# Routing a transformer block's experts by token halves, with the router's product in four column groups

## The chip, the cores and the metric

One NeuronCore of a Trainium2 chip runs the whole program. The metric is the device time of one execution, in microseconds, as the median of several runs.

## The reference

One encoder block over 256 tokens of width 1024, in fp32. The first part (projections, three attention branches, gates) ends in an output projection and a residual sum; the second part is a mixture of 16 experts in four groups, of which each token uses two of one group:

```
x = x + (g_ret * y_ret + g_na * y_na + g_xa * y_xa) @ w_out
t = rmsnorm(x, g_ffn)
grp = top_1(softmax(t @ w_rg + b_rg))                 # 4 groups
in_grp = (t @ w_re + b_re)[grp's 4 experts]
top_w, top_idx = top_2(softmax(in_grp)), weights rescaled to sum 1, times the group's weight
out = sum over the chosen experts e of  weight_e * (silu(t @ w_gate[e]) * (t @ w_up[e])) @ w_down[e]
x = rmsnorm(x + out, g_final)
```

w_gate and w_up are 16 x 1024 x 512, w_down is 16 x 512 x 1024: 100.7 MB of weights in fp32, read once.

## The kernel before

Products of the first part are made in three fp32r matmuls of a high and a low part. ScalarE rounds a tile to its high part, VectorE subtracts to get the low one; the raw weights go through some ten buffers, the converted ones through five ("h").

The stretch of the change begins with the output projection. `wout(q, pts)` (line 868) multiplies a quarter q of the contraction for both token halves (a = 0, 1; 128 tokens each) into PSUM, 12 matmuls of 512 columns. It runs four quarters for the first 512 output columns (n = 0) and four for the second (n = 1). For each half of the columns and of the tokens, `x1_sum` (881) adds the residual on VectorE, `x1_sq` (885) squares on ScalarE for the norm, `x1_T` (889) transposes four 128 x 128 blocks on TensorE, `x1_ev` (894) copies them out on ScalarE, and `logits` (897) multiplies them with the router weights: 128 columns of tokens are the stationary operand, 32 columns of router weights (20 used) the moving one. `x1_rstd` (949) makes 1/rms on VectorE and GpSimd. `seed` (904) multiplies x1 by the identity into the four PSUM accumulators that the experts' results are added to.

Then comes the routing. `route(a)` (1011) is a chain of twelve small VectorE operations for one token half: scale the logits, take the best group, select its experts, take the best two, make a 0/1 mask. The two halves are interleaved (1041). Matmuls with a triangle of ones count positions (1048), and `select(g)` (1105) turns them into a 0/1 matrix of tokens by slots, 64 slots for each of a group's four experts. `gather` (1116) multiplies the normed x1 (a high and a low part, `normed_hi` and `normed_lo`, 977 and 981) with it: 16 matmuls for the high part, 16 for the low one, and ScalarE and VectorE scale the result by the gain into `xg`.

The expert loop `experts` (1286) takes two experts at a time. `gate_up` (1183) makes gate and up products side by side: gate in the array's columns 0 to 63, up in 64 to 127, in plain fp32. Then ScalarE's Silu and VectorE's product write `gs` (1198, 1199), `hidden` (1235) transposes it, `down` (1202) multiplies by w_down, `weigh` (1225) weighs and splits, `scatter` (1244) adds to the accumulators. At the end `finish` (1257) norms and writes out.

Inside this stretch every engine runs its instructions in the order written (`manual_schedule`). Expert weights come by SP's queue in a fixed order of units of 1 MB, each into one of about 20 buffers: `fetch(tag)` (139) issues the next unit into the buffer just released, so an issue waits for the last matmul that reads the buffer. A unit of gate and up weights is 256 rows of both, two transfers of 512 KB with 2 KB runs (`rows_in`, 147; `gate_and_up`, 767). A unit of w_down is 256 rows, with 4 KB runs.

Of the kernel before, what the change touches and what calls it, by code (L numbers as in the profile page):

```python
# [30 lines left out]
def hybrid_encoder_kernel(  # L31
# [694 lines left out]
    V.memset(wr, 0.0)  # L726
    tc.keep_in_program_order(nc.sync.dma_start(wr[:, :, 16:20], w_rg[0].rearrange("(k p) n -> p k n", p=P)))
# [36 lines left out]
    def expert_units():  # L764
        us = []

        def gate_and_up(e, r):
            def go(raw):
                for h, w in ((0, w_gate), (1024, w_up)):
                    rows_in(w[e, r : r + 256])(raw[:, h : h + 1024])  # L770

            return go
# [95 lines left out]
    def wout(q, pts):  # L868
        w = halves.pop(0)
        for a in range(2):  # L870
            ts = slice(a * P, (a + 1) * P)
            for k in range(2):
                kk = 2 * q + k
                PE.matmul(pts[a], m_hi[kk // 4][:, kk % 4, ts], w[k][0], start=kk == 0, stop=False)
                PE.matmul(pts[a], m_hi[kk // 4][:, kk % 4, ts], w[k][1], start=False, stop=False)
                PE.matmul(pts[a], m_lo[kk // 4][:, kk % 4, ts], w[k][0], start=False, stop=kk == KT - 1)
        if not parts:
            hl_tags.remove(w[2])
            fetch(w[2])
# [30 lines left out]
    for q in range(4):  # L910
        if q < 2:
            mt = mixed_T(1, q)
        wout(q, p0)
        if q < 2:
            mixed(1, q, mt)
        feed()
# [6 lines left out]
    rlog = [bank([P, 32]) for _ in range(2)]  # L923
    p1 = [pj([P, 512]) for _ in range(2)]
    xt = [bank([P, 4, P]) for _ in range(2)]
    x1T[0] = tmp([P, 4, 256])
    x1_sum(0, 0, p0)
    x1_sum(0, 1, p0)
    x1_sq(0, 0)
    x1_sq(0, 1)  # L930
    wout(0, p1)
    feed()
    wout(1, p1)
    fetch("A0")
    x1_T(0, 0, xt[0])
    x1_T(0, 1, xt[1])
    feed()
    x1_ev(0, 0, xt[0])
    x1_ev(0, 1, xt[1])
    wout(2, p1)  # L940
    logits(0, 0)
    logits(0, 1)
    feed()
    wout(3, p1)
    xt = [pj([P, 4, P]) for _ in range(2)]
    x1T[1] = tmp([P, 4, 256])
# [7 lines left out]
    x1_sum(1, 0, p1)  # L954
    fetch("E0")
    x1_T(1, 0, xt[0])
    x1_sq(1, 0)
    x1_ev(1, 0, xt[0])
    x1_sum(1, 1, p1)
    x1_rstd(0)  # L960
    x1_T(1, 1, xt[1])
    logits(1, 0)
    x1_sq(1, 1)
    x1_ev(1, 1, xt[1])
    logits(1, 1)
    x1_rstd(1)
    tx.close()
    tpx.close()
    fp = ctx.enter_context(tc.tile_pool(name="fp", bufs=1))
    for tag in ("T0", "T1"):  # L970
        home[tag] = fp
        fetch(tag)
# [13 lines left out]

    for a in range(2):
        for n in range(2):
            normed_hi(a, n)
            seed(x1, a, n)  # L990
    show("x1", x1)
# [19 lines left out]
    def route(a):  # L1011
        V.scalar_tensor_tensor(lgt[:, a, 0:20], rlog[a][:, :20], r2[:, a : a + 1], rb, op0=ALU.mult, op1=ALU.add)
        yield
        V.max(gval[:, a], lgt[:, a, 16:24])
        yield
        V.max_index(gidx[:, a], gval[:, a], lgt[:, a, 16:24])
        yield
        V.tensor_tensor(ohg[:, a], io4, gidx[:, a, 0:1].to_broadcast([P, 4]), op=ALU.is_equal)
        yield
# [6 lines left out]
        yield  # L1026
        V.tensor_reduce(pad[:, a, 0:4], sel[:, a].rearrange("p g e -> p e g"), axis=AX.X, op=ALU.add)
        yield
        V.max(eval_[:, a], pad[:, a])
        yield  # L1030
        V.max_index(eidx[:, a], eval_[:, a], pad[:, a])
        yield
        for i in range(2):
            V.tensor_tensor(oh[:, i, a], io4, eidx[:, a, i : i + 1].to_broadcast([P, 4]), op=ALU.is_equal)
        yield
        V.tensor_add(m4[:, a], oh[:, 0, a], oh[:, 1, a])
        yield
        spread(msk, m4, a)
        yield

    rt = [route(a) for a in range(2)]
    for i in range(16):
        if i < 11:
            next(rt[0])
        if i >= 5:
            next(rt[1])
    pp = bank([P, 3, 16])
    for o, pieces in (
        (pp[:, 0], ((tri, 0),)),
        (pp[:, 1], ((tri, 1), (ones, 0))),  # L1050
        (pp[:, 2], ((ones, 0), (ones, 1))),
    ):
# [10 lines left out]
    e21 = tiny(2, tag="e21")  # L1063
    V.tensor_sub(e21, eval_[:, :, 1], eval_[:, :, 0])
    A.activation(e21, e21, AF.Exp)
    A.activation(warm, e21[:, 0:1], AF.Silu)
    V.tensor_add(posm, posm, pp[:, 0:2])
    cmax = tiny(1, tag="cmax")

    def counts():  # L1070
        V.tensor_reduce(cmax, pp[:, 2], axis=AX.X, op=ALU.max)

# [30 lines left out]
    counts()  # L1103

    def select(g):
        pd = slot("X", [P, 2, 4, SLOTS], F32R)
        for a in range(2):
            V.tensor_tensor(
                pd[:, a],
                posm[:, a, 4 * g : 4 * g + 4].unsqueeze(2).to_broadcast([P, 4, SLOTS]),  # L1110
                iota.unsqueeze(1).to_broadcast([P, 4, SLOTS]),
                op=ALU.is_equal,
            )
        return pd

    def gather(pd, lead=False):
        pts = [bank([P, 2, 256]) for _ in range(4)]

        def part(u, x, first):
            for j in range(2):  # L1120
                ks = slice((2 * u + j) * P, (2 * u + j + 1) * P)
                for a in range(2):
                    PE.matmul(
                        pts[u][:, j],
                        x[:, a, ks],
                        pd[:, a].rearrange("p e s -> p (e s)"),
                        start=first and j + a == 0,
# [298 lines left out]
```

## Time and profile before

| | |
|---|---|
| median of 3 runs | 545.36 us (545.16 to 545.42) |
| the profiled execution | 545.44 us, span 543.5 us |
| PE (TensorE matmuls) busy | 528.5 us, 97% of the span |
| DVE (VectorE) busy | 264.3 us, 49% |
| ACT (ScalarE) busy | 229.0 us, 42% |
| granted TensorE clock, mean | 0.994 of full speed |
| moved by DMA | 159.91 MB, mean 294 GB/s, over 400 GB/s in most slices of the expert loop |

PE's busy time comes from pipelined matmuls whose ends are modelled: the distance between the starts of two matmuls tells more than the duration of one. PEld is the loading of weights into the array. A row of the timeline gives the start in us, the duration, engine, line and operation, output and inputs by the program's names, sizes, how many instructions of the kind are merged (x4), and in brackets how long the engine stood idle before and who released it. Names are cut: "b" and "pj" are PSUM tiles, "C" is x1 or xg, "h", "A", "E", "G", "r" are buffers of weights. L12 is line 12 of the kernel.

### The profile page before, as it was taken

The page shows a single profiled execution, that of the slowest core. Times are in us where ns is not written, and L with a number is a line of the kernel's source. Part 1 is how long each engine was busy: PE and PEld are TensorE (multiplying, and loading weights), DVE is VectorE, ACT ScalarE, POOL GpSimd, SP SyncE. Part 2 cuts the span into 40 slices and gives each one's busy share as a digit, 9 for nine tenths or more (in the row PEclk, how much of TensorE's full clock was granted, in tenths as well). Part 3 has the DMA queues.
Part 4 walks back from the last instruction along what each step waited for, and adds up shares of the span by engine and source line. Part 5 has one row for each costly group of instructions (what it writes and reads, how often), then busy time and mean ns, then how long its engine had stood idle before and what let it go on. Part 6 is the DMA issues. An engine that isn't in the chain of part 4 may idle for free. (4 is left out here: it accounts for less than half of the span.)

```text
span 543.5 us, 7482 instructions
## 1 busy us (share of the span) xinstructions
PE 528.5 (97%) x2912; PEld 359.9 (66%) x2912; DVE 264.3 (49%) x461; ACT 229.0 (42%) x378; POOL 18.5 (3%) x21
## 2 busy tenths in 40 slices
PE   8999999999999999999999999999999999999992
PEld 6999899967778888888888863353435343534340
DVE  6598798995657768384566171130112111210122
ACT  6775566698654464544535261121111111111123
POOL 0005000040000000000000000000000000000000
PEclk9999999999999999999999999999999999999997
DMA  8987778045445799739983799999999999999962
GB/s 302 390 316 233 224 147 256 17 156 163 148 154 189 235 334 301 257 103 403 354 318 151 275 344 330 416 406 418 406 414 409 409 413 407 416 406 418 406 242 81
DMA packets 89815, 159.91 MB, mean 294 GB/s; under 512 B 13104, under 2 KB 27824, under 8 KB 89776
## 3 DMA queue, kind: packets, MB, share of 16 engines
q1 hardware_dynamic: 89056, 158.80, 80.1%
q10 hardware_dynamic: 720, 0.58, 0.3%
q8 instruction: 25, 0.41, 0.3%
q14 instruction: 14, 0.11, 0.1%
HBM read 158.32 MB, written 1.05 MB: 293 GB/s over the span
## 5 line engine op out<-in xcount | busy, mean ns | idle before, releaser
L129 DVE TENSOR_TENSOR h<-r,h 128x1024 fp32r<-128x1024 f32 x58 | 71.2, 1239 | 31.6 <-ACT h L128 31.2
L128 ACT CAST h<-r 128x1024 fp32r<-128x1024 f32 x58 | 60.2, 1048 | 23.4 <-PE pj L308 12.5
L306 PE MATMUL pj<-h,A 128*128 128x512 f32 x160 | 63.1, 394 | 0.0
L308 PE MATMUL pj<-h,A 128*128 128x512 f32 x160 | 62.7, 392 | 0.0
L307 PE MATMUL pj<-h,A 128*128 128x512 f32 x160 | 62.6, 391 | 0.0
L1199 DVE TENSOR_TENSOR gs<-gs,b 64x512 f32<-64x512 f32 x16 | 11.1, 691 | 87.1 <-ACT gs L1198 87.1
L288 PE MATMUL pj<-A,h 128*128 128x256 f32 x160 | 45.7, 286 | 0.0
L290 PE MATMUL pj<-A,h 128*128 128x256 f32 x160 | 45.5, 284 | 0.0
L289 PE MATMUL pj<-A,h 128*128 128x256 f32 x160 | 45.3, 283 | 0.0
L308 PEld LDWEIGHTS pj<-h,A 128*128 128x128 f32 x160 | 30.1, 188 | 6.9 <-issue 0.8
L306 PEld LDWEIGHTS pj<-h,A 128*128 128x128 f32 x160 | 30.1, 188 | 6.7 <-issue 0.4
L307 PEld LDWEIGHTS pj<-h,A 128*128 128x128 f32 x160 | 30.1, 188 | 6.3 <-DVE h L129 0.4
L1230 DVE SCALAR_TENSOR_TENSOR os<-b,c,os 128x512 fp32r<-128x512 f32 x16 | 12.0, 751 | 41.9 <-ACT os L1229 41.0
L1198 ACT ACTIVATE gs<-b 64x512 f32<-64x512 f32 x16 | 9.4, 588 | 51.8 <-PE b L1191 51.8
L288 PEld LDWEIGHTS pj<-A,h 128*128 128x128 f32 x160 | 30.7, 192 | 0.1
L290 PEld LDWEIGHTS pj<-A,h 128*128 128x128 f32 x160 | 30.7, 192 | 0.1
L289 PEld LDWEIGHTS pj<-A,h 128*128 128x128 f32 x160 | 30.7, 192 | 0.1
L129 DVE TENSOR_TENSOR h<-G,h 128x1024 fp32r<-128x1024 f32 x18 | 24.1, 1346 | 10.3 <-ACT h L128 9.8
L1229 ACT ACTIVATE os<-b,c 128x512 fp32r<-128x512 f32 x16 | 11.0, 687 | 40.6 <-PE b L1210 39.7
L1191 PE MATMUL b<-h,C 128*64 128x512 f32 x104 | 24.0, 592 | 0.0
L128 ACT CAST h<-G 128x1024 fp32r<-128x1024 f32 x18 | 18.8, 1049 | 10.6 <-PE pj L308 9.3
L1210 PE MATMUL b<-h,hh 128*64 128x512 f32 x64 | 21.3, 592 | 0.0
(327 smaller groups left out, 1029.3 us busy)
## 6 DMA issues: line engine op xcount, KB each, us to landing
r<-in_w_in_dram SPq DMA_DIRECT2D x20, 1024.0 KB, 5.4
h<-in_w_exp_down_dram SPq DMA_DIRECT2D x10, 1024.0 KB, 11.5
h<-in_w_exp_gate_dram SPq DMA_DIRECT2D x13, 512.0 KB, 11.0
h<-in_w_exp_up_dram SPq DMA_DIRECT2D x13, 512.0 KB, 11.1
r<-in_w_exp_down_dram SPq DMA_DIRECT2D x6, 1024.0 KB, 11.6
A<-in_w_exp_down_dram SPq DMA_DIRECT2D x5, 1024.0 KB, 11.4
r<-in_w_exp_gate_dram SPq DMA_DIRECT2D x9, 512.0 KB, 10.2
r<-in_w_exp_up_dram SPq DMA_DIRECT2D x9, 512.0 KB, 10.3
```

Of the source, the lines that this page charges most:

```text
L128: pin(A.copy(hi, part))
L129: pin(V.tensor_sub(lo, part, hi.bitcast(F32)))
L288: PE.matmul(pt, whi[:, cs], thi[:, k], start=k == 0, stop=False)
L289: PE.matmul(pt, whi[:, cs], tlo[:, k], start=False, stop=False)
L290: PE.matmul(pt, wlo[:, cs], thi[:, k], start=False, stop=k == kn - 1)
L306: PE.matmul(pts[a], thi[:, kk, ts], whi, start=first, stop=False)
L307: PE.matmul(pts[a], thi[:, kk, ts], wlo, start=False, stop=False)
L308: PE.matmul(pts[a], tlo[:, kk, ts], whi, start=False, stop=last)
L1191: PE.matmul(pt[c * 64 : c * 64 + 64], xg[:, k, p % 2 * 2 + i], w[:, 2 * c + j], start=k == 0, stop=k == KT - 1)
L1199: V.tensor_mul(gs[i * 64 : i * 64 + 64], gs[64:128], pt[64:128])
L1210: PE.matmul(pts[n][i * 64 : i * 64 + 64], hh[:, 2 * u + k], ws[i][1][:, k, ns], start=u + k == 0, stop=u + k == 2)
L1230: V.scalar_tensor_tensor(o[:, 1], pt, c, o[:, 0].bitcast(F32), op0=ALU.mult, op1=ALU.subtract)
```

## The change

- The second column half of the output projection goes by token halves: all four quarters for half 0 (with the first half's transposes and logits between them), then quarters 1 to 3 for half 1.
- The router's product swaps its operands: 32 columns of router weights are stationary, 128 tokens move, and the four blocks of a column half go to the four groups of 32 array columns. `bound` copies the four partial sums out (ScalarE) and adds them by one more matmul, which also turns them back.
- `route(0)` is put before `route(1)`, no longer interleaved, and three quarters of half 0's gather are put ahead of `route(1)`. The four PSUM banks of the gather ("lead") hold the logits, the positions and the transposes before. Seeds are cut into 256 columns and put at other places.
- Expert weights are read in 8 KB runs: a unit is 512 rows of gate or of up weights, partition p holding rows 4p to 4p+3, and w_down likewise. `gate_up` takes two units at a time and releases both behind eight matmuls. To match, the normed x1 and the gate/up results are written in permuted order, read at a stride of four elements (`fours`). The gain in that order, `gx`, is loaded in eight small transfers.

The diff, cut:

```
-    def rows_in(src, parts=1):
+    def runs_in(src, parts=1):
         def go(raw):
-            dst = raw.rearrange("p (k n) -> p k n", n=src.shape[1])
+            dst = raw.rearrange("p (k n) -> p k n", n=src.shape[2])
             k = dst.shape[1] // parts
-            for i in range(parts):
-                feeder[0].dma_start(
-                    dst[:, i * k : i * k + k], src[i * k * P : (i + 1) * k * P].rearrange("(k p) n -> p k n", p=P)
-                )
+            for i in range(0, dst.shape[1], k):
+                feeder[0].dma_start(dst[:, i : i + k], src[:, i : i + k])
 
         return go
...
     V.memset(wr, 0.0)
+    gx = cp.tile([P, KT], F32, name="gx")
+    for q in range(4):
+        src = gains.rearrange("(p j) c -> p j c", j=4)
+        for u in range(2):
+            pin(nc.sync.dma_start(gx[q * 32 : q * 32 + 32, 4 * u : 4 * u + 4], src[:, :, 24 + 4 * u + q]))
...
         def gu(e):
-            us.extend(gate_and_up(e, r) for r in range(0, D, 256))
+            for r in (0, 512):
+                us.extend(runs_in(w[e, r : r + 512].rearrange("(p j) n -> p j n", j=4)) for w in (w_gate, w_up))
+
+        def by_four(e):
+            return w_down[e].rearrange("(p k) n -> p k n", k=4)
 
         def dn(*es):
-            for r in (0, 256):
-                us.extend(rows_in(w_down[e, r : r + 256]) for e in es)
+            for k in (0, 2):
+                us.extend(runs_in(by_four(e)[:, k : k + 2]) for e in es)
 
         def dn_cols(e):
             for c in (0, 512):
-                us.append(rows_in(w_down[e, :, c : c + 512], 2 if c and e == NE - 1 else 1))
+                us.append(runs_in(by_four(e)[:, :, c : c + 512], 2 if c and e == NE - 1 else 1))
...
+    def wout(q, pts, w, a, ks=(0, 1)):
+        ts = slice(a * P, (a + 1) * P)
+        for k in ks:
+            kk = 2 * q + k
+            PE.matmul(pts[a], m_hi[kk // 4][:, kk % 4, ts], w[k][0], start=kk == 0, stop=False)
+            PE.matmul(pts[a], m_hi[kk // 4][:, kk % 4, ts], w[k][1], start=False, stop=False)
+            PE.matmul(pts[a], m_lo[kk // 4][:, kk % 4, ts], w[k][0], start=False, stop=kk == KT - 1)
+
+    def used(w):
+        hl_tags.remove(w[2])
+        fetch(w[2])
...
     def logits(n, a):
         for j in range(4):
             k = 4 * n + j
-            PE.matmul(rlog[a], x1T[n][:, j, a * P : (a + 1) * P], wr[:, k], start=k == 0, stop=k == KT - 1)
-
-    acc = [[None, None], [None, None]]
-
-    def seed(base, a, n):
-        acc[a][n] = acc[a][n] or pj([P, 512])
-        PE.matmul(acc[a][n], ident, base[:, a, n * 512 : n * 512 + 512], start=True, stop=False)
+            PE.matmul(
+                sheaf[a][32 * j : 32 * j + 32],
+                wr[:, k],
+                x1T[n][:, j, a * P : (a + 1) * P],
+                start=not n,
+                stop=bool(n),
+            )
+
+    def bound(a):
+        A.copy(sheaves[:, a], sheaf[a])
+        PE.matmul(rlog[a], sheaves[:, a], four, start=True, stop=True)
...
+    lead = [bank([P, 512]) for _ in range(4)]
+    spare = lead[3]
+    rlog = [lead[0][:, 32:64], spare[:, 32:64]]
+    pp = [lead[0][:, 0:16], spare[:, 64:80], spare[:, 80:96]]
+    sheaf = [b[:, 128:256] for b in (lead[0], spare)]
+    sheaves = cp.tile([P, 2, P], F32, name="sheaves")
+    four = cp.tile([P, 32], F32, name="four")
+    for g in range(4):
+        gs = slice(32 * g, 32 * g + 32)
+        A.copy(four[gs], ident[gs, gs])
+    xt = [b.rearrange("p (j t) -> p j t", j=4) for b in lead]
...
+    acc = [[p0[a], p1[a]] for a in range(2)]
+
+    def seed(base, a, n, hs=(0, 1)):
+        for h in hs:
+            cs = slice(h * 256, h * 256 + 256)
+            PE.matmul(acc[a][n][:, cs], ident, base[:, a, n * 512 + h * 256 : n * 512 + h * 256 + 256], start=not h, stop=False)
+
+    for n in range(2):
+        x1T[n] = tmp([P, 4, 256])
...
+    def fours(t):
+        return t.rearrange("q (p j) -> q j p", j=4)
+
+    def by_p(t):
+        return t.rearrange("q (j p) -> q j p", j=4)
+
     def normed_hi(a, n):
         ns = slice(n * 512, n * 512 + 512)
-        A.activation(x1_hi[:, a, ns], x1[:, a, ns], AF.Copy, scale=r2[:, a : a + 1])
+        A.activation(by_p(x1_hi[:, a, ns]), fours(x1[:, a, ns]), AF.Copy, scale=r2[:, a : a + 1])
 
     def normed_lo(a, n):
         ns = slice(n * 512, n * 512 + 512)
         V.scalar_tensor_tensor(
-            x1_lo[:, a, ns], x1[:, a, ns], r2[:, a : a + 1], x1_hi[:, a, ns].bitcast(F32), op0=ALU.mult, op1=ALU.subtract
+            by_p(x1_lo[:, a, ns]),
+            fours(x1[:, a, ns]),
+            r2[:, a : a + 1],
+            by_p(x1_hi[:, a, ns].bitcast(F32)),
+            op0=ALU.mult,
+            op1=ALU.subtract,
         )
...
+    def settled(a):
+        V.scalar_tensor_tensor(posm[:, a], msk[:, a], 1e6, pp[a], op0=ALU.mult, op1=ALU.add)
+
+    def chosen(pd, g, a):
+        V.tensor_tensor(
+            pd[:, a],
+            posm[:, a, 4 * g : 4 * g + 4].unsqueeze(2).to_broadcast([P, 4, SLOTS]),
+            iota.unsqueeze(1).to_broadcast([P, 4, SLOTS]),
+            op=ALU.is_equal,
+        )
+
+    def part(pt, u, x, pd, a, first, last):
+        pt = pt.rearrange("p (j c) -> p j c", j=2)
+        for j in range(2):
+            k = 2 * u + j
+            PE.matmul(
+                pt[:, j],
+                x[:, a, k * P : (k + 1) * P],
+                pd[:, a].rearrange("p e s -> p (e s)"),
+                start=first and not j,
+                stop=last and j == 1,
+            )
...
+    for a in range(2):
+        x1_sum(0, a, p0)
+        x1_sq(0, a)
+    ws = [halves.pop(0)]
+    for a in range(2):
+        wout(0, p1, ws[0], a)
+    used(ws[0])
+    feed()
+    ws += halves
+    wout(1, p1, ws[1], 0)
+    for a in range(2):
+        x1_T(0, a, xt[a])
+        x1_ev(0, a, xt[a])
+    wout(2, p1, ws[2], 0)
+    wout(3, p1, ws[3], 0)
+    for a in range(2):
+        logits(0, a)
+    x1_sum(1, 0, p1)
+    x1_sq(1, 0)
+    x1_rstd(0)
+    wout(1, p1, ws[1], 1)
+    used(ws[1])
+    fetch("A0")
+    x1_T(1, 0, xt[2])
+    x1_ev(1, 0, xt[2])
+    for n in range(2):
+        normed_hi(0, n)
+        normed_lo(0, n)
+    wout(2, p1, ws[2], 1)
+    used(ws[2])
+    logits(1, 0)
+    wout(3, p1, ws[3], 1, (0,))
+    bound(0)
+    wout(3, p1, ws[3], 1, (1,))
+    used(ws[3])
+    fetch("E0")
+    x1_sum(1, 1, p1)
+    x1_sq(1, 1)
+    route(0)
+    x1_rstd(1)
+    seed(x1, 0, 0)
+    x1_T(1, 1, xt[1])
+    x1_ev(1, 1, xt[1])
+    seed(x1, 1, 0)
+    logits(1, 1)
+    PE.matmul(pp[0], tri, msk[:, 0], start=True, stop=True)
+    pd0 = slot("X", [P, 2, 4, SLOTS], F32R)
+    settled(0)
+    chosen(pd0, 0, 0)
+    bound(1)
+    tx.close()
+    tpx.close()
+    fp = ctx.enter_context(tc.tile_pool(name="fp", bufs=1))
+    for tag in ("T0", "T1"):
+        home[tag] = fp
+        fetch(tag)
+    for u in range(3):
+        for x in (x1_hi, x1_lo):
+            part(lead[u], u, x, pd0, 0, x is x1_hi, False)
+    for n in range(2):
+        normed_hi(1, n)
+    route(1)
+    for o, pieces in ((pp[1], ((tri, 1), (ones, 0))), (pp[2], ((ones, 0), (ones, 1)))):
         for i, (l, a) in enumerate(pieces):
-            PE.matmul(o, l, msk[:, a], start=i == 0, stop=i == len(pieces) - 1)
-    posm = cp.tile([P, 2, 16], F32, name="posm")
-    V.tensor_scalar(posm, msk, 1e6, -1e6, op0=ALU.mult, op1=ALU.add)
+            PE.matmul(o, l, msk[:, a], start=i == 0, stop=i == 1)
+    settled(1)
+    counts()
+    chosen(pd0, 0, 1)
+    part(spare, 3, x1_hi, pd0, 0, True, False)
+    part(spare, 3, x1_lo, pd0, 0, False, False)
+    for u in range(4):
+        part(lead[u], u, x1_hi, pd0, 1, False, False)
+    for a in range(2):
+        seed(x1, a, 1)
     gneg = tiny(2, tag="gneg")
     V.tensor_scalar_mul(gneg, gval[:, :, 0], -1.0)
+    e21 = tiny(2, tag="e21")
+    V.tensor_sub(e21, eval_[:, :, 1], eval_[:, :, 0])
+    for n in range(2):
+        normed_lo(1, n)
+    for u in range(4):
+        part(lead[u], u, x1_lo, pd0, 1, False, True)
...
+            for x in () if done else (x1_hi, x1_lo):
+                for a in range(2):
+                    part(pt, u, x, pd, a, x is x1_hi and a == 0, x is x1_lo and a == 1)
+            pt = pt.rearrange("p (j c) -> p j c", j=2)
+            if bool(u % 2) != bool(done):
                 for j in range(2):
                     k = 2 * u + j
                     A.activation(
-                        xg[:, k].rearrange("p e s -> p (e s)"), pt[:, j], AF.Copy, scale=gt[:, 3, k : k + 1]
+                        xg[:, k].rearrange("p e s -> p (e s)"), pt[:, j], AF.Copy, scale=gx[:, k : k + 1]
...
     def gate_up(xg, i, p, gs, between=None):
         pt = bank([P, DFF])
         for u in range(2):
-            for h in range(2):
-                tag, w = take(DFF)
-                for j in range(2):
-                    k = 4 * u + 2 * h + j
-                    for c in range(2):
-                        PE.matmul(
-                            pt[c * 64 : c * 64 + 64], xg[:, k, p % 2 * 2 + i], w[:, 2 * c + j], start=k == 0, stop=k == KT - 1
-                        )
+            ws = [take(DFF) for _ in range(2)]
+            for k in range(4 * u, 4 * u + 4):
+                for c in range(2):
+                    PE.matmul(
+                        pt[c * 64 : c * 64 + 64], xg[:, k, p % 2 * 2 + i], ws[c][1][:, k % 4], start=k == 0, stop=k == KT - 1
+                    )
+            for tag, _ in ws:
                 fetch(tag)
             if between and not u:
                 between()
         gs = gs or keep([P, DFF], "gs")
-        A.activation(gs[64:128], pt[0:64], AF.Silu)
-        V.tensor_mul(gs[i * 64 : i * 64 + 64], gs[64:128], pt[64:128])
+        A.activation(by_p(gs[64:128]), fours(pt[0:64]), AF.Silu)
+        V.tensor_mul(by_p(gs[i * 64 : i * 64 + 64]), by_p(gs[64:128]), fours(pt[64:128]))
```

## Rows read from the trace of the kernel before

**Rows 1.** Windows: us; busy us (instructions) by engine, clock, DMA share, GB/s.
```profile
298.00:324.47 26.47, 25.29 (x146) 20.45 (x144) 12.98 (x49) 11.31 (x26) 1.10 (x2) 1.00 0.81 302
324.47:543.50 219.03, 208.54 (x1075) 86.03 (x1074) 37.27 (x76) 39.67 (x76) 1.08 (x2) 0.99 0.95 374
```
**Rows 2.** Waits of TensorE's weight loads from 324 us: us, times, longest.
```profile
PEld b L1210 <- DMA T<-in_w_exp_gate_dram: 0.6, 2, 0.3
```
**Rows 3.** Timeline of TensorE in the expert loop.
```profile
340.73 1.89 PE L1191 MATMUL b<-h,C 128*64 128x512 f32 x8
342.55 0.66 PE L1239 MATMUL b<-ident,gs 128*128 128x128 f32 x4
343.13 1.94 PE L1191 MATMUL b<-B,C 128*64 128x512 f32 x8
```
**Rows 4.** Windows in the weight stream and at its end.
```profile
340.00:344.00 4.00, 4.00 (x22) 1.35 (x20) 0.54 (x1) 0.59 (x1) 0.00 (x0) 1.00 1.03 423
...
356.00:360.00 4.00, 4.00 (x26) 2.28 (x24) 0.08 (x1) 0.21 (x1) 0.00 (x0) 1.00 1.05 404
...
524.00:526.00 2.00, 2.00 (x12) 0.72 (x10) 0.88 (x2) 0.86 (x2) 0.00 (x0) 1.00 0.27 107
```
**Rows 5.** Timeline of TensorE at the last weights.
```profile
528.76 1.94 PE L1221 MATMUL b<-h,hh 128*64 128x512 f32 x8
```
**Rows 6.** Timeline of TensorE from the output projection to the expert loop.
```profile
304.19 1.03 PE L892 MATMUL b<-ident,C 128*128 128x128 f32 x8
...
304.98 0.48 PE L874 MATMUL pj<-h,E 128*128 128x512 f32 x1
...
307.81 1.87 PE L900 MATMUL b<-wr,t 128*128 128x32 f32 x16
...
309.51 0.47 PE L874 MATMUL pj<-h,E 128*128 128x512 f32 x1
...
312.13 0.40 PE L876 MATMUL pj<-h,E 128*128 128x512 f32 x1
...
315.65 3.68 PE L906 MATMUL pj<-C,ident 128*128 128x512 f32 x8
...
320.27 2.36 PE L1123 MATMUL b<-X,C 128*128 128x256 f32 x16 [0.83 <-DVE X L1108]
...
324.48 1.94 PE L1191 MATMUL b<-B,C 128*64 128x512 f32 x8
```
**Rows 7.** Timeline of VectorE in the same stretch.
```profile
312.57 0.69 DVE L883 TENSOR_TENSOR C<-pj,t 128x512 f32<-128x512 f32 x1 [0.70 <-PE pj L876]
...
314.90 0.24 DVE L1012 SCALAR_TENSOR_TENSOR lgt<-b,r,rb 128x20 f32<-128x20 f32 x1 [0.50 <-PE b L900]
...
317.24 0.17 DVE L1004 TENSOR_TENSOR msk<-ohg,m 128x16 bf16<-128x16 f32 x1
...
318.48 0.17 DVE L1004 TENSOR_TENSOR msk<-ohg,m 128x16 bf16<-128x16 f32 x1
...
319.48 0.19 DVE L1067 TENSOR_TENSOR posm<-posm,b 128x32 f32<-128x32 f32 x1 [0.47 <-PE b L1054]
...
320.38 2.73 DVE L983 SCALAR_TENSOR_TENSOR E<-C,r,C 128x512 fp32r<-128x512 f32 x4
```
**Rows 8.** Timeline of ScalarE, emptying the gather's banks.
```profile
323.63 1.79 ACT L1146 ACTIVATE C<-b,gt 128x256 f32<-128x256 f32 x4 [2.37 <-PE b L1123]
```
**Rows 9.** Timeline of SP's queue, projection weights.
```profile
208.91 0.37 SPq L121 DMA_DIRECT2D B<-in_w_in_dram  x1
```
**Rows 10.** Waits of all engines from 180 to 300 us.
```profile
ACT h L128 <- PE pj L308: 28.5, 22, 3.0
```
**Rows 11.** Timeline of all engines at the last gate/up product.
```profile
521.12 0.59 ACT L1198 ACTIVATE gs<-b 64x512 f32<-64x512 f32 x1 [3.12 <-PE b L1191]
521.74 0.69 DVE L1199 TENSOR_TENSOR gs<-gs,b 64x512 f32<-64x512 f32 x1 [3.55 <-ACT gs L1198]
522.72 0.46 PE L1239 MATMUL b<-ident,gs 64*128 64x64 f32 x4
```

More of the change, by code (lines that the diff above doesn't have):

```diff
@@ L866, in hybrid_encoder_kernel @@
     x1T = {}
[L868 to L879, printed above, removed]
+    def wout(q, pts, w, a, ks=(0, 1)):
[8 more added lines that the diff above has]
+        fetch(w[2])
     def x1_sum(n, a, pts):
@@ L912, in hybrid_encoder_kernel @@
             mt = mixed_T(1, q)
-        wout(q, p0)
+        w = halves.pop(0)
+        for a in range(2):
+            wout(q, p0, w, a)
         if q < 2:
             mixed(1, q, mt)
+        if not parts:
+            used(w)
         feed()
@@ L921, in bank @@
         return psc.tile(shape, F32, tag="b", name=nm("b"))
-    rlog = [bank([P, 32]) for _ in range(2)]
-    p1 = [pj([P, 512]) for _ in range(2)]
[L925 to L946, printed above, removed]
+    lead = [bank([P, 512]) for _ in range(4)]
[9 more added lines that the diff above has]
+    xt = [b.rearrange("p (j t) -> p j t", j=4) for b in lead]
+    p1 = [pj([P, 512]) for _ in range(2)]
+    acc = [[p0[a], p1[a]] for a in range(2)]
[5 more added lines that the diff above has]
+        x1T[n] = tmp([P, 4, 256])
     r2 = cp.tile([P, 2], F32, name="r2")
@@ L983, in normed_lo @@
         V.scalar_tensor_tensor(
-            x1_lo[:, a, ns], x1[:, a, ns], r2[:, a : a + 1], x1_hi[:, a, ns].bitcast(F32), op0=ALU.mult, op1=ALU.subtract
-        )
[L987 to L991, printed above, removed]
+            by_p(x1_lo[:, a, ns]),
[4 more added lines that the diff above has]
+            op1=ALU.subtract,
+        )
     gval = cp.tile([P, 2, 8], F32, name="gval")
@@ L1041, in hybrid_encoder_kernel @@
[L1041 to L1052, printed above, removed]
-        for i, (l, a) in enumerate(pieces):
-            PE.matmul(o, l, msk[:, a], start=i == 0, stop=i == len(pieces) - 1)
-    posm = cp.tile([P, 2, 16], F32, name="posm")
@@ L1056, in hybrid_encoder_kernel @@
-    V.tensor_scalar(posm, msk, 1e6, -1e6, op0=ALU.mult, op1=ALU.add)
+    posm = cp.tile([P, 2, 16], F32, name="posm")
+    V.tensor_scalar_add(iota, iota, 1e6)
+    def settled(a):
[7 more added lines that the diff above has]
+        )
@@ new lines, in part, with counts @@
+    def part(pt, u, x, pd, a, first, last):
[9 more added lines that the diff above has]
+            )
+    cmax = tiny(1, tag="cmax")
+    def counts():
+        V.tensor_reduce(cmax, pp[2], axis=AX.X, op=ALU.max)
@@ L1062, in hybrid_encoder_kernel @@
         A.activation(gex, lgt[:, a, 16:20], AF.Exp, bias=gneg[:, a : a + 1], accum_out=gsum[:, a : a + 1])
-    e21 = tiny(2, tag="e21")
-    V.tensor_sub(e21, eval_[:, :, 1], eval_[:, :, 0])
     A.activation(e21, e21, AF.Exp)
[L1066 to L1071, printed above, removed]
+    show("x1", x1)
     def weights():
@@ L1107, in select, with gather @@
         for a in range(2):
[L1108 to L1112, printed above, removed]
-            )
-        return pd
-    def gather(pd, lead=False):
-        pts = [bank([P, 2, 256]) for _ in range(4)]
-        def part(u, x, first):
-            for j in range(2):
-                ks = slice((2 * u + j) * P, (2 * u + j + 1) * P)
-                for a in range(2):
-                    PE.matmul(
[L1124 to L1127, printed above, removed]
-                        stop=not first and j + a == 2,
-                    )
-        if lead:
-            for u in range(4):
-                part(u, x1_hi, True)
-            for n in range(2):
-                for a in range(2):
-                    normed_lo(a, n)
+            chosen(pd, g, a)
+        return pd
+    def gather(pd, pts=None):
+        done = pts
+        pts = pts or [bank([P, 512]) for _ in range(4)]
         xg = slot("C1", [P, KT, 4, SLOTS])
@@ L1139, in gather @@
             pt = pts[u]
-            if not lead:
-                part(u, x1_hi, True)
-            part(u, x1_lo, False)
-            if u % 2:
+            for x in () if done else (x1_hi, x1_lo):
+                for a in range(2):
+                    part(pt, u, x, pd, a, x is x1_hi and a == 0, x is x1_lo and a == 1)
+            pt = pt.rearrange("p (j c) -> p j c", j=2)
+            if bool(u % 2) != bool(done):
                 for j in range(2):
@@ L1284, in finish, with experts @@
                 (nc.sync, nc.scalar)[a].dma_start(out[0, a * P : (a + 1) * P, n * 512 : n * 512 + 512], o)
-    def experts(pd, first, lead=False):
+    def experts(pd, first, lead=None):
         st = {}
@@ L1306, in experts @@
         xg = gather(pd, lead)
+        if lead:
+            A.activation(warm, e21[:, 0:1], AF.Silu)
         for p in range(NP):
@@ L1339, in experts @@
         finish(1)
-    pd0 = select(0)
-    experts(pd0, weights, True)
+    experts(pd0, weights, lead)
     run.close()
```

41 lines of the change are left out of this document (1 added, 40 removed).

## The prediction

> **What bounds the kernel now.** I read the stages first: the windows view splits the span where the expert loop starts, at 324.47 us. From there to the end TensorE is busy 208.54 of 219.03 us, and the missing 10.5 us are the last normalisation and the output transfer [rows 1]. The DMA share is just as high, so the view of waits decides between the two: the largest wait of TensorE's weight loads for a transfer is 0.6 us in two pieces [rows 2]. The timeline agrees: a unit of eight matmul instructions in two column groups takes 1.72 us (0.215 each) and the next stands right behind it [rows 3]. So the expert loop is TensorE's, and the weights arrive in time, in the end with little to spare: the last transfers run out near 524.6 us (share 0.27 of the window from 524), and the last weights are used from 528.76 [rows 4, 5]. The loop's length is fixed by its matmuls, and the change leaves their number alone. What can move the end is when the first gate/up matmul starts (324.48), and a wait inside the loop or at its tail.
>
> Second, the stretch before it, from 298: TensorE is busy 25.29 of 26.47 us [rows 1], so at most 1.2 us of idle time lies here. Its timeline: the last projection matmul issues at 312.13; call its end, 312.36, E. The first gate/up matmul follows 12.12 us after E [rows 6]. In these 12.12 us VectorE adds the residual (312.57), routes both token halves interleaved (314.90 to 318.65), and the gather's 32 matmuls run from 320.27 to 324.48, 0.132 each [rows 6, 7].
>
> **The change, part by part.** All times below are of the profiled execution: 545.44 us, which is 543.5 of span and 1.94 around it. It stands 0.08 above the median of the runs, 545.36.
>
> *TensorE up to E.* Removed: the logits of the first column half, 307.81 to 309.51, 1.70 us [rows 6]. Their second half stood after E, and there the chain below runs on VectorE. Moved ahead of E: four transposes of the first token half, at 0.79 for eight (304.19 to 304.98), 0.40 [rows 6]. Added ahead of E: three of the four new logit sets, one `bound` matmul, and two changes into narrow column groups and back. A set is eight instructions of 128 columns in four groups. A 512-column pass takes 0.43 in a group with two groups side by side [rows 3], so a 128-column pass takes 0.107: a set costs 0.21 if all four groups overlap and 0.86 if none do. I take 0.3, near the lower end, since rows 3 show full overlap of two groups, with a little for the loads. A change into the full array and back is seen at 342.55: the unit before it is due to end at 340.73 + 1.72 = 342.45, so 0.10 is lost going in; four transposes then need 0.40 and the next unit starts 0.58 later, so 0.18 is lost coming back [rows 3]; 0.28 a round trip. The Trainium skill says in "TensorEngine Tiling (Array Packing)", Key Properties, that changing the tiling mode drains TensorE; by that rule four column groups are not free between full-array matmuls. The row agrees, with 0.28; without the rule the sum below would be 0.56 smaller. `bound` is two instructions with 128-column weights; the old logits show 0.106 for such a one, so 0.25 with its handover. Sum: 3 x 0.3 + 2 x 0.28 + 0.40 + 0.25 - 1.70 = +0.41: E comes 0.41 later (bounds +0.14 and +2.1, from the set alone).
>
> *From E to the first gate/up matmul.* The new order puts both routes on VectorE one behind the other. From E: 0.21 to the residual add, 0.69 for it [rows 7]; route of half 0, alone, 2.5 (314.90 to 317.41); its positions through TensorE and back, 0.35; position and selection of one half, 0.55 (add, count and both selections take 0.9, 319.48 to 320.38); route of half 1, 2.5; positions 0.4; position, count, selection 0.65; 0.05 between the first two. That is 7.9, and the old order starts its gather at 320.27, also 7.9 after E. Behind it TensorE has 16 gather matmuls, 2.1, plus 0.1 of four others that don't all fit under the selection, and between them two seeds. Four seeds are eight instructions from 315.65, 0.43 each [rows 6], so two are 1.72. They cover the low parts of half 1 on VectorE (two of 0.68) [rows 7], which need only 0.5 of it past the high parts. Total 11.8. Then the first bank must be emptied before the gate/up product can reuse it: two ScalarE copies of 0.45 [rows 8], 0.15 to reach them, against 0.79 of matmuls still running: +0.3. So 12.15 after E, against 12.12: +0.03. What is gained by gathering three quarters of half 0 early (12 matmuls, 1.6 us) and by ending the seeds' block before the position counts is paid back by 1.25 us of routes no longer interleaved (5.0 against 3.75) and by seeds now standing between the parts.
>
> *Weights in 8 KB runs, two units taken at a time.* TensorE does not wait for weights, so a faster stream buys nothing by itself. It pays for a later one: the first slots come free after two units, 3.44 instead of 1.72 us, and A0 and one more slot are released some 4 us later than now, behind twelve more projection matmuls at 0.24 (eleven steps from 309.51 to 312.13) [rows 6] and a block of logits. The stream moved 404 GB/s with 2 KB runs and 423 with 4 KB runs [rows 4]: 0.116 us per unit of 1.05 MB. From 324.47 on 374 GB/s over 219 us are 82 MB [rows 1], two thirds of it gate and up weights: 52 units, 6.0 us in all. I take at least that for 8 KB runs; the lower bound is no gain. Even then some 3.9 us of slack at the end cover a restart about 3 us later. Cost 0.
>
> *Small loads of the gains.* Eight loads are put on SP's queue ahead of the router weights. At about 0.4 us an issue (0.37 in the row of 208.91) [rows 9] they push what follows by some 3 us: the router weights, which VectorE scales in its order, so that its conversions behind them wait, and the next projection weights. Cover: between 180 and 300 ScalarE's conversions wait 28.5 us, 22 times, for TensorE to free one of the five converted buffers [rows 10], so four buffers of twelve matmuls at 0.24, 11 us of work, are converted ahead. Cost 0; without that cover 3 us.
>
> *Strided operands.* The split activations and the gate/up products are read at a stride of four elements. The trace has no such instruction of this size. The bounds are no cost, and a doubled time per element; I take none in the sum and price the other end as a rival.
>
> Sum: +0.41 + 0.03 = +0.44, so 545.44 + 0.44 = **545.9 us**.
>
> **The rivals.**
> *Strided operands cost, and the kernel gets slower.* Place: the gate/up product of the last pair, and the splits ahead of E. At the tail ScalarE's 0.59 and VectorE's 0.69 end at 522.43, and the transposes that read them start at 522.72 [rows 11]; 0.29 is free. The part that grows with the elements: VectorE takes 0.24 for 20 and 0.69 for 512 [rows 7], so 0.45; ScalarE 0.45 for 256 and 0.59 for 512 [rows 8, 11], so 0.28. Doubled, they add 0.73, of which 0.44 comes through. Ahead of E two high parts on ScalarE, 0.28 longer each, delay the copy inside `bound(0)`, by some 0.4 behind what is free there. With the +0.44: 545.44 + 1.28 = 546.7. It decides from 0.29 us for the pair of instructions on. In the pairs before, 3.44 us of matmuls stand between the product and its use, and nothing shows. No row stands nearer to one bound than to the other, hence a large chance. The Trainium skill speaks for it: in "Advanced Engine Details and Errata", Memory Cachelines, it says that SBUF wants at least two hits on a 16-byte line, and a stride of four fp32 gives one; no row here shows it.
> *The four groups do not overlap.* Sets of 0.86: three before E add 1.7: 547.6. Rows 3 speak against it.
> *The path closes up.* TensorE runs dense from E on: the 1.2 us of idle time goes, and the logits in all fall from 3.5 (twice about 1.7) to 4 x 0.3 + 3 x 0.28 + 2 x 0.25 = 2.5. That is -2.2 at most; with some of it kept by VectorE, -1.5: 543.9. For it speaks that the work on TensorE does shrink; against it, two routes of 2.5 in a row on VectorE.
> *The stream binds after all.* Then 8 KB runs pay up to 6.0 of the 545.9: about 540. The missing waits speak against it.
>
> **How the numbers follow.** A difference of about 0.2% (1.1 us) is what a measurement of this kernel can tell from none. The forecast, no difference, has 0.42, with its own range from 545.0 to 546.4. Strided operands 0.28 and groups that don't overlap 0.08 make slower 0.36. The closed path 0.20 and the stream 0.02 make faster 0.22. The range goes from just below the closed path, 543.7, to the groups' case, 547.7.
>
> **What would show it.** In the changed profile: the last projection matmul 0.2 to 0.7 us later than 312.13; a logit set of about 0.3; the first gate/up matmul between 324.2 and 325.5, and the same distance from it to the end as now, 219.0. The strided instructions at 0.6 to 0.7 us clear that rival, at 0.9 to 1.2 they make it. If the first gate/up matmul stands before 323.4, my chain from E is wrong; if that distance shrinks, the loop was not TensorE's.

## The result

The changed kernel takes 549.57 us (four runs, 548.46 to 550.08), the kernel before 545.39: a ratio of 1.0073, interval 1.0057 to 1.0089. The forecast, 545.9 with a range up to 547.7, was wrong. The profiled execution took 549.44 us, 4.0 more than that of before. A table of five stretches, read from the starts in the timelines, shows where:

| stretch | before | after | difference | predicted |
|---|---|---|---|---|
| start of the span to the projection's second column half | 298.75 | 301.26 | +2.51 | no term |
| from there to the last projection matmul | 13.38 | 14.37 | +0.99 | +0.41 |
| to the first gate/up matmul | 12.35 | 12.04 | -0.31 | +0.03 |
| to the issue of the last output transfer | 212.82 | 212.80 | -0.02 | 0 |
| to the end of the span | 6.20 | 7.03 | +0.83 | no term |

Over half of the loss lies ahead of 298 us, in a part of the kernel that the change leaves alone but for eight small loads, and a fifth behind the issue of the last transfer.

### The profile page after: what moved, and what is told of

Its sections match the earlier page's. It is cut to its first block, busy times and chain, and to the rows that moved or that the text cites. A ratio compares the mean times of both kernels' runs of the same rounds, so it can differ in the third digit from the quotient of the medians.

```text
span 547.5 us, 7447 instructions
## 1 busy us (share of the span) xinstructions
PE 527.2 (96%) x2924; PEld 358.7 (66%) x2924; DVE 266.8 (49%) x462; ACT 232.5 (42%) x384; POOL 18.5 (3%) x21
## 5 line engine op out<-in xcount | busy, mean ns | idle before, releaser
L286 PE MATMUL pj<-A,h 128*128 128x256 f32 x160 | 45.7, 286 | 0.0
L1231 PE MATMUL b<-h,C 128*64 128x512 f32 x104 | 39.6, 594 | 0.0
L1231 PE MATMUL b<-B,C 128*64 128x512 f32 x64 | 29.0, 596 | 0.2 <-ACT C L1188 0.2
L1231 PE MATMUL b<-G,C 128*64 128x512 f32 x64 | 29.0, 596 | 0.0
```

The source lines that it names most:

```text
L286: PE.matmul(pt, whi[:, cs], thi[:, k], start=k == 0, stop=False)
L1231: PE.matmul(pt[c * 64 : c * 64 + 64], xg[:, k, p % 2 * 2 + i], ws[c][1][:, k % 4], start=k == 0, stop=k == KT - 1)
```

## The profile after

TensorE's timeline of the changed kernel (start, duration, operation, sizes); it answers to [rows 6]:

```profile
301.26 0.39 PE L872 MATMUL pj<-h,A 128*128 128x512 f32 x1
...
308.73 0.39 PE L874 MATMUL pj<-h,E 128*128 128x512 f32 x1
309.04 0.64 PE L899 MATMUL b<-t,wr 128*32 128x128 f32 x16
309.62 0.50 PE L872 MATMUL pj<-h,A 128*128 128x512 f32 x1
...
312.74 0.40 PE L874 MATMUL pj<-h,E 128*128 128x512 f32 x1
313.07 0.43 PE L899 MATMUL b<-t,wr 128*32 128x128 f32 x8
313.42 0.50 PE L872 MATMUL pj<-h,E 128*128 128x512 f32 x1
313.76 0.39 PE L873 MATMUL pj<-h,E 128*128 128x512 f32 x1
313.99 0.40 PE L874 MATMUL pj<-h,E 128*128 128x512 f32 x1
314.84 0.41 PE L909 MATMUL b<-four,sheaves 128*128 128x32 f32 x2 [0.46 <-ACT sheaves L908]
315.08 0.47 PE L872 MATMUL pj<-h,E 128*128 128x512 f32 x1
...
315.63 0.39 PE L874 MATMUL pj<-h,E 128*128 128x512 f32 x1
...
323.66 1.12 PE L1038 MATMUL b<-X,C 128*128 128x256 f32 x8
...
327.67 0.64 PE L1231 MATMUL b<-B,C 128*64 128x512 f32 x1 [0.22 <-ACT C L1188]
```

The windows of the two stretches, answering to [rows 1] (window and its length; busy time of five engines, with how many instructions; granted clock, DMA share, GB/s):

```profile
301.20:327.67 26.47, 23.75 (x154) 18.66 (x153) 14.46 (x48) 13.40 (x31) 1.11 (x2) 1.00 0.70 275
327.67:547.50 219.83, 208.50 (x1074) 86.03 (x1074) 37.57 (x77) 41.02 (x78) 1.08 (x2) 0.98 0.91 376
```

From the projection's second column half to the first gate/up matmul TensorE is busy 23.69 of 26.41 us, before 24.55 of 25.73 (the window of [rows 1] starts 0.75 us earlier than that): the shorter logits are paid for in waits. With the projection's pace of 0.23 behind the matmul before them, two logit sets take 0.66 (308.96 to 309.62) and one takes 0.45 (312.97 to 313.42). So a set takes 0.21, the prediction's figure for a full overlap of the four groups, and a change of groups and back 0.24. `bound` waits 0.46 for ScalarE's copy. ScalarE and VectorE of the same kernel, at that place, show why:

```profile
312.31 2.32 ACT L969 ACTIVATE C<-C,r 128x512 fp32r<-128x512 f32 x2
314.53 0.26 ACT L908 COPY sheaves<-b 128x128 f32<-128x128 f32 x1
...
313.57 2.23 DVE L973 SCALAR_TENSOR_TENSOR E<-C,r,C 128x512 fp32r<-128x512 f32 x2 [2.78 <-ACT C L969]
316.06 0.69 DVE L882 TENSOR_TENSOR C<-pj,t 128x512 f32<-128x512 f32 x1 [0.26 <-PE pj L874]
...
322.98 0.42 DVE L1027 TENSOR_TENSOR X<-posm,iota 128x256 fp32r<-128x256 f32 x1
```

A strided split takes 1.16 on ScalarE (two in 2.32) and 1.12 on VectorE; before it took 0.64 (four in 2.56 from 314.57) and 0.68 [rows 7]. The copy, whose logits were ready by 313.5, stands behind two of them. At the tail the strided pair, which reads PSUM, takes what it took before [rows 11]:

```profile
524.31 0.59 ACT L1239 ACTIVATE gs<-b 64x512 f32<-64x512 f32 x1 [3.12 <-PE b L1231]
524.93 0.69 DVE L1240 TENSOR_TENSOR gs<-gs,b 64x512 f32<-64x512 f32 x1 [3.55 <-ACT gs L1239]
```

Of the early loss of 2.51, 2.4 is one wait. The waits of TensorE's weight loads in the first 60 us of the changed kernel:

```profile
PEld at L237 <- DVE t L232: 2.7, 1, 2.7
```

The same wait before:

```profile
PEld at L239 <- DVE t L234: 0.3, 1, 0.3
```

VectorE's instruction there (32.45 after, 29.96 before) stands behind conversions of weights that had landed later: in these 60 us ScalarE's conversions wait 2.1 us for the loads into r, before 1.1. The windows of the first loads and of the loop, after:

```profile
12.00:16.00 4.00, 4.00 (x20) 3.30 (x19) 2.76 (x6) 2.59 (x5) 0.00 (x0) 1.00 1.10 349
22.00:34.00 12.00, 9.47 (x78) 9.22 (x77) 6.32 (x9) 6.30 (x9) 0.72 (x1) 1.00 1.10 345
340.00:520.00 180.00, 180.00 (x930) 74.87 (x927) 28.03 (x52) 29.52 (x54) 0.00 (x0) 1.00 1.01 420
```

And before:

```profile
12.00:16.00 4.00, 4.00 (x20) 3.30 (x19) 3.08 (x5) 2.91 (x5) 0.00 (x0) 1.00 1.09 385
22.00:34.00 12.00, 11.91 (x98) 11.66 (x97) 8.68 (x13) 6.77 (x11) 0.72 (x1) 1.00 1.08 385
340.00:520.00 180.00, 180.00 (x942) 75.28 (x940) 28.20 (x54) 29.64 (x55) 0.00 (x0) 1.00 1.04 411
```

The same loads in the same order, with all DMA engines busy in both (share 1.1), move 349 GB/s instead of 385. What differs is where they land. The pool of constants comes first in SBUF and the large buffers behind it. The change adds three constants: `gx` (32 bytes per partition), `sheaves` (1024) and `four` (128), 1184 in all, or 4 x 256 + 160. In the kernel before, the buffers that take 146 of the 158 MB of loads start on multiples of 256 bytes; after, they start 160 past one. (The other large ones, among them the two buffers T0 and T1 of expert weights, lie 128 past a multiple before and 32 past one after.) That became theory A.

## The experiments

**e1, e3 and e5: the kernel before, its buffers shifted** by 32, 64 and 128 bytes through the width of a constant that it has anyway:

```
-    nhalf = cp.tile([P, 16], F32, name="nhalf")
+    nhalf = cp.tile([P, 24], F32, name="nhalf")     # e1; 32 in e3, 48 in e5
```

> The kernel before with one constant tile 32 bytes wider, so that every large SBUF buffer starts 32 bytes past a multiple of 256 instead of on one; nothing else changes. In the changed kernel the same buffers start 160 past one, and its first loads, which are instruction for the instruction those of before, moved 349 GB/s at 12 to 16 us against 385. Theory A, the address of the buffers: the early loads move about 349 GB/s here too, TensorE waits some 2.5 us near 31 us, and the time is 547.7 to 548.7, two thirds of the changed kernel's loss or more without one line of the change. Theory B, the changed code itself (its small loads, its longer program) or chance between launches: 385 GB/s, and 545.4 plus or minus 0.3.

> The kernel before with the same constant tile 64 bytes wider: the large buffers start 64 bytes past a multiple of 256. It tells, if theory A (the address of the buffers) holds, how far a buffer must be aligned. Only to 64 bytes: 545.4, early loads at 385 GB/s. To 128 or 256 bytes: 547.7 to 548.7, early loads near 349 GB/s. Theory B, the changed code or chance: 545.4.

> The kernel before with one constant tile 128 bytes wider, so that its large buffers start 128 bytes past a multiple of 256. Shifts of 32 and 64 bytes cost 8.6 and 7.3 us. If a buffer must start on a multiple of 128, this costs nothing: 545.3, 385 GB/s at 12 to 16 us, 411 in the expert loop. If it must start on a multiple of 256: 552 to 554, 349 GB/s at 12 to 16 us and 394 in the loop.

Measured: e1 553.88 us, ratio 1.0158 (1.0144 to 1.0172); e3 552.57, 1.0145 (1.0128 to 1.0162); e5 551.62 (two runs), 1.0114 (1.0096 to 1.0133), 0.4 below the 552 to 554 of its second case. Theory A holds, and a multiple of 128 is not enough. That a shift would cost 8.6, three times what it costs the changed kernel, was not expected. The windows of e1:

```profile
12.00:16.00 4.00, 4.00 (x19) 3.34 (x18) 2.76 (x5) 2.61 (x4) 0.00 (x0) 1.00 1.09 352
...
340.00:520.00 180.00, 176.40 (x896) 72.60 (x892) 28.04 (x52) 29.51 (x54) 0.00 (x0) 1.00 1.04 394
```

The second column shows the rest: in the expert loop TensorE is busy 176.40 of 180, so with 394 GB/s the weights no longer arrive in time, and from the first gate/up matmul to the last output issue it takes 218.73 instead of 212.82. From 327 us on TensorE's weight loads wait 4.8 us, three times, for w_down in the buffers r; before, the largest wait for a transfer was 0.6 [rows 2]. In e5 it is the same at 397 GB/s:

```profile
12.00:16.00 4.00, 4.00 (x19) 3.31 (x18) 2.73 (x6) 2.56 (x5) 0.00 (x0) 1.00 1.10 349
340.00:520.00 180.00, 177.75 (x901) 73.23 (x897) 28.03 (x52) 29.48 (x54) 0.00 (x0) 1.00 1.04 397
```

**e2: the changed kernel, aligned again.**

```
-    gx = cp.tile([P, KT], F32, name="gx")
+    gx = cp.tile([P, 4 * KT], F32, name="gx")[:, :KT]      # 1280 bytes in all
```

> The changed kernel with the tile gx 96 bytes wider, so that the large buffers start on multiples of 256 bytes again (1280 bytes higher than in the kernel before). Theory A, the address: the early loads are back at 385 GB/s, the wait near 31 us goes, what is left is the change's own stretch, +0.5, and perhaps 0.8 behind the last output transfer: 545.6 to 546.8. Theory B, the changed code or chance: 549.0 to 550.0, as the changed kernel.

Measured: 546.91 us, ratio to before 1.0032 (1.0020 to 1.0043), 2.66 below the changed kernel: 0.1 above theory A's range and 2.1 below theory B's. Its windows:

```profile
12.00:16.00 4.00, 4.00 (x20) 3.30 (x19) 2.98 (x5) 2.90 (x4) 0.00 (x0) 1.00 1.09 384
22.00:34.00 12.00, 11.74 (x97) 11.48 (x96) 8.74 (x13) 6.60 (x11) 0.72 (x1) 1.00 1.09 386
340.00:520.00 180.00, 180.00 (x942) 75.37 (x940) 28.35 (x54) 30.20 (x56) 0.00 (x0) 1.00 1.01 424
```

The early loads are back at 384 and the projection's second column half starts at 298.74, as before. In the loop the 8 KB runs lose little to the bad address (420 against 424 GB/s), and nothing of the time hangs on it.

**e4: the routing order alone, aligned.** 8 KB runs, strided operands and small loads are undone.

```
-            for r in (0, 512):
-                us.extend(runs_in(w[e, r : r + 512].rearrange("(p j) n -> p j n", j=4)) for w in (w_gate, w_up))
+            us.extend(gate_and_up(e, r) for r in range(0, D, 256))
...
-        A.activation(by_p(x1_hi[:, a, ns]), fours(x1[:, a, ns]), AF.Copy, scale=r2[:, a : a + 1])
+        A.activation(x1_hi[:, a, ns], x1[:, a, ns], AF.Copy, scale=r2[:, a : a + 1])
```

> The changed kernel's routing order alone: the weights again by rows of 128 in runs of 2 and 4 KB, taken one unit at a time, the gains from their first place (no small loads), no strided operands; the large buffers on multiples of 256 bytes. Theory S, strided operands cost on the path: the last projection matmul comes some 0.4 earlier after the first one of its unit than in the changed kernel (14.0 instead of 14.4 us behind the first matmul of that projection), bound's copy does not wait behind two takes of 1.17, and the time is 0.3 to 0.6 below that of the aligned changed kernel. Theory N, they are hidden: the two kernels agree within 0.2. A theory that the 8 KB runs pay: this one is slower than the aligned changed kernel by more than 0.3.

Measured: 545.24 us, ratio to before 0.9999 (0.9990 to 1.0008). The routing order is worth nothing, and the 8 KB runs with what belongs to them cost 1.67 on aligned buffers. That is more than theory S had, since the end of the span shrank back too: 6.16 behind the last issue, against 7.12 in e2. Up to the last projection matmul it took 13.64 against 14.38 in e2, to the first gate/up matmul 12.05 in both.

**e8: long runs, but flat splits.** The splits of the normalised x1 are contiguous again; the permutation of the columns that goes with the long runs is left out.

```
-        A.activation(by_p(x1_hi[:, a, ns]), fours(x1[:, a, ns]), AF.Copy, scale=r2[:, a : a + 1])
+        A.activation(x1_hi[:, a, ns], x1[:, a, ns], AF.Copy, scale=r2[:, a : a + 1])
```

> The changed kernel with its large buffers on multiples of 256 bytes, as in e2, in which the split of the normalised activations reads and writes contiguous columns; the permutation of the columns is left out, so gate and up products pair columns wrongly. All else, 8 KB runs, the strided gate/up products of each pair and the small loads, stays. Theory S, the strided splits are what delays the end of the projections: the takes are back at 0.64 and 0.68 instead of 1.17 and 1.12, the last projection matmul comes 9.55 us after the first transpose instead of 10.29, and the time is 0.7 below e2: 546.2. Theory R, the long runs or the small loads do it: 10.29 and 546.9.

Measured: 546.55 us, 0.36 below e2 with runs scattered over 1.5 us; so the time alone would not tell. The profile does: 13.65 to the last projection matmul, as in e4, and the copy of `bound` goes at once behind short splits:

```profile
309.60 1.34 ACT L969 ACTIVATE C<-C,r 128x512 fp32r<-128x512 f32 x2
310.85 0.27 ACT L908 COPY sheaves<-b 128x128 f32<-128x128 f32 x1
...
310.36 1.41 DVE L973 SCALAR_TENSOR_TENSOR E<-C,r,C 128x512 fp32r<-128x512 f32 x2 [2.27 <-ACT C L969]
```

Theory S holds: the 0.73 are the strided splits', not the runs' or the small loads'.

**e7 and e10: code that is not run.** Behind the experts stands a loop that these inputs never enter. e7 adds 24 loads on SyncE in its body, e10 62 copies on ScalarE; both have aligned buffers.

```
             feeder[0] = nc.scalar
+            for _ in range(62):
+                A.copy(warm, nhalf[:, 0:1])
```

> The changed kernel with its large buffers on multiples of 256 bytes, as in e2, and 24 small loads on SyncE in the body of the loop that no execution of these inputs enters. Nothing that runs is changed, only how far the code behind the loop lies for SyncE. In the changed kernel and in e2 the span ends 7.0 to 7.1 us after the last output transfer is issued, with a fetch of instructions in its last half microsecond, in the kernel before and in e4 6.2, without it. Theory F, the end of SyncE's code falls across a boundary of what one fetch brings: the distance is 6.1 to 6.3 here and the time 545.9 to 546.2, 0.9 below e2. Theory G, the fetch is another engine's, or it hangs on what runs: 7.1 and 546.9, as e2.

> As e7, but the instructions that no execution enters are 62 copies on ScalarE, as many as the longer runs took out of that loop's body there; the end of ScalarE's code lies again where it lies in the kernel before, to 4 instructions. Theory H, the fetch at the end of the span is ScalarE's, and hangs on where its code behind the skipped loop falls: last output issue to end of span 6.1 to 6.3 instead of 7.1, no fetch in the last half microsecond, time 546.0 to 546.3. Theory G, it hangs on something else: 7.1 and 546.9, as e2 and e7.

Measured: e7 547.14 us, and 7.23 from the last issue to the end: theory F fell. e10 546.29 us, 0.62 below e2, and 6.32: theory H holds. The last microsecond of e2:

```profile
544.10:544.60 0.50, 0.00 (x0) 0.00 (x0) 0.00 (x0) 0.00 (x0) 0.00 (x0) 0.50 0.00 0
544.60:545.10 0.50, 0.00 (x0) 0.00 (x0) 0.00 (x0) 0.00 (x0) 0.00 (x0) 0.50 0.04 16
```

And of e10:

```profile
542.90:543.40 0.50, 0.00 (x0) 0.00 (x0) 0.00 (x0) 0.00 (x0) 0.00 (x0) 0.50 0.00 0
543.40:543.90 0.50, 0.00 (x0) 0.00 (x0) 0.00 (x0) 0.00 (x0) 0.00 (x0) 0.50 0.00 0
```

The 16 GB/s in half a microsecond are one packet of 8 KB, on a queue that the profile calls instruction. In its last 6.5 us e2 has four such packets, the kernel before and e10 three. The changed kernel issues fewer transfers in the skipped body (279 instructions of ScalarE instead of 341) and has 4 instructions more ahead of it, so ScalarE's code behind it moved by 58 instructions, to where it needs one fetch more.

**e9 and e11: is the routing order worth anything?** e9 puts the first half's second seed into the 0.87 us in which TensorE of e4 waits for the second mask (318.46 to 319.33; the profile counts 0.72 of it as idle). e11 besides starts the first routing ahead of the last residual add.

```
             part(lead[u], u, x, pd0, 0, x is x1_hi, False)
+    seed(x1, 0, 1)
...
-    for a in range(2):
-        seed(x1, a, 1)
+    seed(x1, 1, 1)
```

> e4 (the routing order alone, aligned, 545.24) with one move: the first token half's second seed is issued behind the early gather parts instead of behind the second half's high parts. In e4 TensorE is idle from about 318.46 to 319.33 there, waiting for the second routing. If that idle time can be used, the first gate/up matmul comes 0.8 earlier (11.2 instead of 12.05 behind the last projection matmul) and the time is 544.4. If the low parts on VectorE, done near 321.7, or the emptying of the first bank hold the gate/up product instead, the gain is under 0.3: 545.0 or more.

> e9 (routing order alone, aligned, second seed moved: 544.38) in which the first three instructions of the first half's routing go ahead of the last residual add on VectorE, into 0.8 us in which VectorE waits for the last projection matmul. If VectorE's chain of residual, routing, position and routing sets the start of the expert loop, the first gate/up matmul comes 0.3 to 0.6 earlier than in e9 (10.6 to 10.9 behind the last projection matmul) and the time is 543.8 to 544.1. If the second half's logits through ScalarE and TensorE, ready some 3.4 after that matmul, or TensorE's gather set it, it gains under 0.15: 544.3 or more.

Measured: e9 544.38 us, ratio to before 0.9983 (0.9974 to 0.9992), with 11.20 from the last projection matmul to the first gate/up matmul. e11 544.23, 0.9978 (0.9969 to 0.9987), with 10.85. That distance shrank by 0.35 as its first theory had it, but the time by 0.15, between the two theories' figures. TensorE of e4 at the gap:

```profile
318.22 0.40 PE L1033 MATMUL b<-X,E 128*128 128x256 f32 x2
319.33 0.17 PE L1110 MATMUL b<-msk,tri 128*128 128x16 bf16 x1 [0.72 <-DVE msk L989]
```

And of e9:

```profile
317.96 0.40 PE L1033 MATMUL b<-X,E 128*128 128x256 f32 x2
318.20 1.03 PE L947 MATMUL pj<-C,ident 128*128 128x256 f32 x4
319.06 0.17 PE L1111 MATMUL b<-msk,tri 128*128 128x16 bf16 x1
```

Both are faster than the kernel before, by 0.2%, with the weights by rows and aligned buffers.

## Why the prediction was wrong

- **The step that failed** is the choice of what can move: "What can move the end is when the first gate/up matmul starts (324.48), and a wait inside the loop or at its tail", with a sum that begins at 298 and takes all that lies ahead as unchanged. Three new constants moved the buffers of the weights off their multiples of 256 bytes: 2.66 of the 4.2 us (the changed kernel against e2), 2.51 of it in the early wait. The sum had no such term, and no rival had this mechanism.
- **"Small loads of the gains ... Cost 0"** was right of the loads and wrong of their tile. They take SyncE longer than the estimated 3 us, eight of 0.60 (median) from 201.1 to 208.5, but the projection's second column half starts at 298.74 in e2 with them and at 298.82 in e4 without. The cover held. The tile's own 32 bytes leave a sum of 1184, which 96 more bytes mend.
- **"Strided operands ... I take none in the sum"** was the wrong end. The rival had the size (1.17 and 1.12 lie in its 0.9 to 1.2) and one of its two places: ahead of E it costs 0.73 (e2 against e4, and e8), where the rival had 0.4. At the tail it costs nothing: there the source is PSUM and the pair takes what it took before. The rival's 546.7 lies near e2's 546.91 by luck: it had 0.44 at the tail and 0.44 for the routing order, which cost nothing, and lacked 0.92 at the end of the span.
- **TensorE up to E**: +0.41 predicted, +0.26 in e4, where nothing else is in it. A set came at 0.21 against 0.3, and a change of groups and back at 0.24 against 0.28, so the sets with their changes take 1.11 where 1.46 stood; the other terms came 0.20 dearer together. The Trainium skill says that changing the tiling mode drains TensorE ("TensorEngine Tiling (Array Packing)", Key Properties); the trace agrees, with these 0.24.
- **From E to the gate/up matmul**: +0.03 predicted, -0.31 measured. VectorE's chain ends at 323.40 (322.98 and 0.42), 7.5 after the projection's end (315.86), where I had 7.9: the steps between the routes come back faster. TensorE is then still at what is left of the first half's gather, so the second half's starts at 323.66, 7.8 after that end, where I had 8.0. From there it takes 4.0, where I had 4.15.
- So the routing order with its two terms gave -0.04 (13.64 and 12.05 in e4 against 13.38 and 12.35) where +0.44 stood, and e4 lies in the forecast's range for "no difference". For the part that I had looked at the verdict was right and the sum 0.48 too high.
- **8 KB runs, cost 0**: right in the loop, 212.80 against 212.82. The rate rose from 411 to 424 when aligned, and nothing waits for it. That the stream has little slack was right as well: in e1, with short runs at 394 GB/s, it binds and costs 5.91 in the loop. The changed kernel has the same kind of bad address and loses nothing there, at 420 GB/s with long runs. (By the prediction's own rows the slack at the end is 528.76 - 524.6 = 4.2, not 3.9; nothing hangs on it.)
- **The end of the span**: +0.83, again without a term; e10 takes back 0.80 of e2's 0.92 in the profile and 0.62 in the medians.

## What to carry to other kernels

Before costing a change, add up the bytes per partition of every new tile that is allocated ahead of the transfers' targets, and, where these targets start on multiples of 256, pad the sum to a multiple of 256. In the kernel before, and in e2 and e4, T0 and T1 lie 128 off a multiple; what moving them alone would give was not run. Split a measured difference by anchors over the whole span, also ahead of and behind the edited code, before explaining it from the edit. A strided read of SBUF costs where someone waits for its engine: ask which instruction stands behind it in that engine's order.

## What the runs showed of the hardware

- **SBUF address of a transfer's target.** Off a multiple of 256 bytes by 32, 64, 128 or 160, loads with packets of about 1 KB move 349 to 352 GB/s instead of 385, whatever the distance. With 16 engines at work that is, worked out from 1550 packets of 1.54 MB at 385 and 1401 of 1.39 MB at 349, 41.3 against 45.7 ns a packet (4 us x 16, by the packets). In the loop, with 2.3 KB a packet, it is 90 against 95 ns (before, 31854 packets of 74.00 MB; e1, 30206 of 70.94). So it looks like a fixed price of 4 to 5 ns a packet, and long runs feel it least (420 against 424). The Trainium skill, "DMA: Bandwidth & Descriptors", How a descriptor splits into AXI transactions, says that a transaction must start on a multiple of 256 bytes and that a descriptor that does not start on one fetches unused bytes. The trace agrees on the 256, here for the address that is written to. An estimate from that page's count of beats: 1 KB would grow by 1 in 32 at an offset of 32 and by 5 in 32 at 160; the measured loss is about 9% at both. What the price consists of stays open, as does whether the source's address matters.
- **Stride of four fp32 in SBUF.** 512 elements: ScalarE 0.67 flat (e8: two in 1.34) against 1.16, VectorE 0.70 (e8: two in 1.41) against 1.12. The Trainium skill, "Advanced Engine Details and Errata", Memory Cachelines, says that at least two hits on a 16-byte line are needed, and that one line per access costs; the trace agrees. Read from PSUM with that stride, on 64 partitions, and written to SBUF flat, 0.59 and 0.69 stay as they were; whether PSUM or the fewer partitions spare them was not run.
- **Code that is skipped has an address too.** One fetch of 8 KB at the very end is worth 0.8 us (6.32 in e10 against 7.12 in e2), and comes or goes with 62 instructions that are never run.
